# Six small experts a layer, and gate and up weights loaded in runs of four rows a partition

## The chip, the cores and the metric

The kernel runs on one core of a Trainium2 chip. The metric is the device time of one execution in microseconds. TensorE (PE) multiplies, VectorE (DVE), ScalarE (ACT) and GpSimd (POOL) do the elementwise work, and SyncE (SP) issues most of the DMAs.

## What is computed

Two layers of a decoder trunk over 512 tokens of width 1024. Each layer has a token mixer (an mLSTM beside sliding-window attention) and then a mixture of 16 experts, of which each token uses two. The change is in the experts alone:

```python
def _grouped_moe(h, w_router, router_bias, w_gate, w_up, w_down):
    ...
    gates = jnp.sum(jax.nn.one_hot(idx, N_EXPERTS, dtype=jnp.float32) * wts[..., None], axis=1)
    gates = gates.astype(h.dtype)
    y = jnp.zeros_like(t)
    for e in range(N_EXPERTS):
        act = jax.nn.silu(t @ w_gate[e]) * (t @ w_up[e])
        y = y + gates[:, e:e + 1] * (act @ w_down[e])
    return y.reshape(b, s, d)
```

`w_gate` and `w_up` are (layer, 16, 1024, 512), `w_down` is (layer, 16, 512, 1024), all float32: 6 MB an expert, 96 MB a layer.

## The kernel before

**One loop over experts.** `moe` runs positions 0 to 15 (line 1917). Each expert sees only the rows routed to it, gathered by an indirect DMA on POOL (`gather`, line 1395). Position 0 uses rows that are at hand; 1 to 15 have a tile `X` of up to 128 rows, one row a partition. Positions 3 to 14 are filled at run time: `order_experts` sorts these twelve experts by their row counts, and the ones with the fewest rows go to the positions in `SMALL`, the others to the rest (`RANK`, `perm`). What does not fit a position (more than 128 rows, or more than 64 at a small one) is left to an overflow block behind the loop. On these inputs it runs in layer 1 alone, for one expert with 146 rows.

**Large and small.** A small position works on 64 rows with plain float32 products: `gateup_small` computes gate and up side by side in two column groups of 64 (`gu`, line 1472), `down_small` the two halves of the down projection likewise (`downs`, line 1498). A large position works on 128 rows in three passes: every weight chunk is split into a high part (ACT, line 1548) and a low part (DVE, line 1549), and `mm3` (lines 116 to 118) sums three products. Its down projection is split in the same way if the position is in `DN` (`split_down`, lines 1457 and 1458), else it is plain float32 (line 1605).

**Order.** For each e the code writes gate and up of e, with the transposes of the previous expert's activations (`aT`) between their halves; then `turn(e + 1)`, which transposes the next expert's gathered rows to `XT` on PE, with `X` as the loaded operand and the identity as the moving one (line 1450 small, 1515 large); then down of e - 1. When a small expert follows one in `DN`, `gateup_small` splits two of that expert's four down blocks early. At e = 14 both down(13) and down(14) are written. A scheduler places the instructions of each engine from this order and its own estimates.

**Loads.** `up_gate` and `dn` list six chunks of 1 MB an expert (128 partitions of 2048 floats), gate and up of the next expert ahead of down of this one. They go through a ring of 12 buffers (`rot`, line 1366); SP issues a chunk when its buffer is free (`load`, line 1381). A chunk of gate or up holds 512 rows of 512 floats: partition p gets rows p, 128 + p, 256 + p and 384 + p, four runs of 2 KB. A down chunk holds 256 rows of 1024 floats, two runs of 4 KB.

Of the kernel before, what the change touches and what calls it, by code (L numbers as in the profile page):

```python
# [48 lines left out]
PQ = 2  # L49
SORTED = range(3, 15)  # L50
NSORT = len(SORTED)
SMALL = (4, 6, 8, 10, 12)
RANK = {}
for _e in SORTED:
    RANK[_e] = SMALL.index(_e) if _e in SMALL else len(SMALL) + sum(1 for _f in SORTED if _f < _e and _f not in SMALL)
DN = (1, 3, 5, 7, 9, 11, 13)
FR = 2
NPI = 2
MP = ((5, 2), (5, 2))
# [20 lines left out]
def tile_trunk(ctx, tc, x, c, w_ada, b_ada, w_norm1, w_in, conv_w, conv_b, b_igate, b_fgate, w_mnorm,  # L80
# [3 lines left out]
    V, A, G, T, SP = nc.vector, nc.scalar, nc.gpsimd, nc.tensor, nc.sync  # L84
# [13 lines left out]
    def ps(name="ps"):  # L98
        return pp.tile([128, 512], F32, tag="ps", name=name)
# [20 lines left out]
    def queue(*ins):  # L120

        for a, b in zip(ins, ins[1:]):
            tc.add_manual_dep(b.ins, a.ins.name, mybir.DependencyInfo(mybir.DependencyClass.NoSync,
                                                                      mybir.DependencyReason.DATA), reason="queue")
# [8 lines left out]
    ident = con.tile([128, 128], F32, name="ident")  # L133
# [1199 lines left out]
    def moe(l, raw2, rt):  # L1333
# [7 lines left out]
        X = [mp.tile([128, D], F32, name=f"X{i}", bufs=1) for i in range(2)]  # L1341
# [8 lines left out]
        regs = {}  # L1350

        def block(w, e, r0, nr):

            def f():
                if e not in RANK:
                    return w[l, e, r0:r0 + nr, :].rearrange("(a p) n -> p a n", p=128)
                if e not in regs:
                    r = RANK[e]
                    regs[e] = nc.values_load(perm[:, r:r + 1], engines=[ET.SP], min_val=SORTED[0], max_val=SORTED[-1])
                return w[l, ds(regs[e], 1), r0:r0 + nr, :].rearrange("o (a p) n -> p (o a) n", p=128)  # L1360
            return f, nr // 128

        def up_gate(e):
# [20 lines left out]
        def pair_of_chunks():  # L1384
            load(nch["got"] + len(rot))
            nch["got"] += 2
            return [loaded.popleft(), loaded.popleft()]

        def col(e):

            return SORTED[0] + RANK[e] if e in RANK else e

        def gather(e):
            n, c = 64 if e in SMALL else 128, col(e)
            G.indirect_dma_start(out=X[e % 2][:n], out_offset=None, in_=h2d[l],  # L1395
                                 in_offset=bass.IndirectOffsetOnAxis(ap=gidx0[:n, e - 1:e] if e < 3 else gidx[:n, c:c + 1], axis=0),
                                 bounds_check=S - 1, oob_is_err=False)
# [32 lines left out]
        def order_places():  # L1430

            V.memset(sml, 0.0)
            V.tensor_scalar(sml[:, sorted_], rank[:, :NSORT], float(len(SMALL)), None, op0=OP.is_lt)
            pr = oscr[:, :2 * TB * NE].rearrange("p (a b) -> p a b", b=NE)
# [8 lines left out]

        stt = {}

        def turn_small(e):
            XT = mpx.tile([128, D], F32, tag="XT", name="XT", bufs=2)[:, :512]
            p = ps("XT")
            for i in range(8):
                T.transpose(p[:, i * 64:(i + 1) * 64], X[e % 2][:64, i * 128:(i + 1) * 128], ident[:64, :64])  # L1450
            A.copy(XT, p)
            stt["XT", e] = XT.rearrange("p (a b) -> p a b", a=8)

# [7 lines left out]
        def gateup_small(e, mid):  # L1461

            XT = stt["XT", e]
            p = ps("gu")
            for half in range(2):
                if half and mid is not None:
                    mid()
                chs = pair_of_chunks()
                for i in range(4):
                    kb = 4 * half + i  # L1470
                    for g in range(2):
                        stt["gl"] = T.matmul(p[g * 64:g * 64 + 64], XT[:, kb], chs[g][:, i], start=kb == 0, stop=kb == KB - 1)  # L1472
            if e - 1 in DN:
                stt["wd", e - 1] = pair_of_chunks()
                stt["sd", e - 1] = [split_down(e - 1, fb) for fb in range(2)]
                stt["early"] = stt["sv"]
            a_ = mp.tile([128, DE], F32, name="act")
            A.activation(a_[64:128], p[0:64], AF.Silu)
            stt["mul", e] = V.tensor_mul(a_[0:64], p[64:128], a_[64:128])
            stt["act", e] = a_  # L1480
# [26 lines left out]
        def turn(e, XT=None):  # L1507
            if e in SMALL:
                return turn_small(e)
            if XT is None:  # L1510
                XT = [mpx.tile([128, D], F32R, tag="XT", name=n, bufs=2).rearrange("p (a b) -> p a b", a=8) for n in ("XTh", "XTl")]
            for q in range(2):
                p = ps("XT")
                for i in range(4):
                    T.transpose(p[:, i * 128:(i + 1) * 128], X[e % 2][:, (4 * q + i) * 128:(4 * q + i + 1) * 128], ident)  # L1515
                h_ = XT[0][:, 4 * q:4 * q + 4].rearrange("p a b -> p (a b)")
                A.copy(h_, p)
                o = V.tensor_sub(XT[1][:, 4 * q:4 * q + 4].rearrange("p a b -> p (a b)"), p, h_)
                if "early" in stt:
                    queue(stt.pop("early"), o)  # L1520
            stt["XT", e] = XT
# [30 lines left out]
        def gateup(e, mid=None):  # L1552
            if e in SMALL:
                return gateup_small(e, mid)
            XT = stt["XT", e]
            pg, pu = ps("gate"), ps("up")
            for half in range(2):
                if half and mid is not None:
                    mid()
                chs = [None] * 2 if e == 0 and half == 0 else pair_of_chunks()  # L1560
                for p, ch in zip((pg, pu), chs):
                    for j in range(2):
                        wh, wl = first.pop(0) if first else pair(ch, j)
                        for a in range(2):
                            kb = 4 * half + 2 * j + a
                            stt["gl"] = mm3(p, XT[0][:, kb], XT[1][:, kb], wh[:, a], wl[:, a], kb == 0, kb == KB - 1)
            a_ = mp.tile([128, DE], F32, name="act")
            A.activation(a_, pg, AF.Silu)
            stt["mul", e] = V.tensor_mul(a_, pu, a_)
            stt["act", e] = a_  # L1570

        def turn_act(e):
            if e in SMALL:
                return turn_act_small(e)
            a_ = stt["act", e]
            p = ps("aT")
            for i in range(4):
                T.transpose(p[:, i * 128:(i + 1) * 128], a_[:, i * 128:(i + 1) * 128], ident)
            if e in DN:
                aT = wsp.tile([128, D], F32R, tag="acc", name="aT", bufs=1).rearrange("p (k a b) -> p k a b", k=2, a=4)  # L1580
                h_, l_ = [aT[:, k].rearrange("p a b -> p (a b)") for k in range(2)]
                A.copy(h_, p)
                V.tensor_sub(l_, p, h_)
                stt["aT", e] = aT
                return
            aT = wsp.tile([128, D], F32, tag="acc", name="aT", bufs=1)[:, :512].rearrange("p (a b) -> p a b", a=4)
            A.copy(aT.rearrange("p a b -> p (a b)"), p)
            stt["aT", e] = aT

        def down(e):  # L1590
# [7 lines left out]
            for fb in range(4):  # L1598
                if e in DN:
                    wh, wl = sd.pop(0) if sd else split_down(e, fb)  # L1600
                for q in range(2):
                    if e in DN:
                        mm3(pd[q], aT[:, 0, fb], aT[:, 1, fb], wh[:, q], wl[:, q], fb == 0, fb == 3)
# [87 lines left out]
        def over_chunk(e, i, pool):  # L1691
            v = pool.tile([128, 2048], F32, tag="raw", name="oW")
            if i:
                G.tensor_copy(v[:, 0:2], g2[:, 0:2])
            w, r0, nr = ((w_gate_e, 0, 512), (w_up_e, 0, 512), (w_gate_e, 512, 512), (w_up_e, 512, 512),
                         (w_down_e, 0, 256), (w_down_e, 256, 256))[i]
            a = nr // 128
            SP.dma_start(v.rearrange("p (a b) -> p a b", a=a),
                         w[l, ds(e, 1), r0:r0 + nr, :].rearrange("o (a p) n -> p (o a) n", p=128))
            return v.rearrange("p (a b) -> p a b", a=a)  # L1700

        def over_block(chs, first=[], mid=None):
# [206 lines left out]
        a, v = turn_first(splits)  # L1909
# [57 lines left out]
        with none.Else():  # L1967
            with tc.If(n0 == 1) as one:
                tail(True)
            with one.Else():  # L1970
                V.tensor_scalar(ovl, ovl, 1.0, None, op0=OP.add)
                with tc.For_i(0, n0, 1):
                    e = over_rows()
# [4 lines left out]
                    for t in range(TB):  # L1978
                        for i in range(2):
                            p = ps("rows")  # L1980
# [182 lines left out]
```

## Time and profile before

| | us |
|---|---|
| median of 3 runs | 1422.01 (1420.73 to 1426.65) |
| the profiled execution | 1422.47 |
| its span in the trace | 1420.5 |
| PE busy | 1329.5 (94%) |
| DVE busy | 1005.1 (71%) |
| ACT busy | 678.4 (48%) |
| POOL busy | 204.8 (14%) |
| DMA, mean over the span | 257 GB/s |

The busy shares are means over the whole span. The experts of layer 0 lie at 420 to 712 us, those of layer 1 some 669 us later with the same pattern; the rest is the mixers and projections. The rows below are all from layer 0's experts but one.

### The profile page before, as it was taken

The numbers are of one execution on the slowest core, as the hardware profiler recorded it, in microseconds if no ns is written. First come the engines' busy times: TensorE is split into PE (matmuls) and PEld (weight loads), VectorE is DVE, ScalarE is ACT, GpSimd is POOL, SyncE is SP. The second block draws the span as 40 slices with busy tenths as digits, with TensorE's granted clock in tenths as the row PEclk, the third lists the DMA queues.
The fourth block names the chain that finished last, engine by engine and source line by source line (L and its number), as shares of the span: only waits on it lengthen the run. The fifth ranks groups of instructions, "written<-read, shape, count | busy, mean of one in ns | idle before, by whom it ended". The sixth has DMA issues, their size and how long they took to land.

```text
span 1420.5 us, 18468 instructions
## 1 busy us (share of the span) xinstructions
PE 1329.5 (94%) x6407; PEld 975.3 (69%) x6407; DVE 1005.1 (71%) x1941; ACT 678.4 (48%) x1184; POOL 204.8 (14%) x250
## 2 busy tenths in 40 slices
PE   2999999999989999999989999999998999999894
PEld 2776777778876756656568777777887666665662
DVE  5687756778679856767767566656958966766767
ACT  4345345454236645545356335435524655554552
POOL 7500020010011111110230000001001111211033
PEclk8999999999999999999999999999999999999997
DMA  9565465576868999999744434456577899999982
GB/s 312 202 219 177 133 246 178 178 232 184 294 218 286 360 376 390 376 370 395 281 158 149 148 97 142 149 194 176 184 261 250 290 351 389 382 375 384 392 317 84
DMA packets 166498, 365.08 MB, mean 257 GB/s; under 512 B 10549, under 2 KB 41517, under 8 KB 166136
## 3 DMA queue, kind: packets, MB, share of 16 engines
q1 hardware_dynamic: 152928, 327.71, 65.5%
q0 software_dynamic: 12752, 33.92, 7.0%
q10 hardware_dynamic: 712, 2.14, 0.5%
q8 instruction: 54, 0.88, 0.2%
q14 instruction: 52, 0.43, 0.1%
HBM read 346.27 MB, written 26.78 MB: 263 GB/s over the span
## 4 chain that ended last, share of the span: by engine, by line
PE 80%; DVE 11%; DMA 5%; issue 2%; ACT 1%; another core or an unknown queue 0%; SPq 0%; POOL 0%; DVEq 0%; ACTq 0%; POOLq 0%
PE winT L116 7%; PE winT L118 6%; PE winT L117 6%; PE gu L1472 5%; PE down L1605 3%; PE gate L117 3%; PE gate L118 3%; PE up L117 3%; PE gate L116 3%; PE up L118 3%; PE up L116 3%; PE downs L1498 2%; PE out L116 2%; PE out L118 2%; PE out L117 2%; DMA raw<-in_w_ada_dram 2%
## 5 line engine op out<-in xcount | busy, mean ns | idle before, releaser
L1548 ACT CAST wh<-raw 128x1024 fp32r<-128x1024 f32 x168 | 175.3, 1051 | 95.8 <-PE gate L118 65.6
L1549 DVE TENSOR_TENSOR wl<-raw,wh 128x1024 fp32r<-128x1024 f32 x168 | 201.5, 1223 | 23.5 <-ACT wh L1548 22.9
L116 PE MATMUL winT<-hh,wh 128*128 128x512 f32 x416 | 168.3, 405 | 0.5 <-DVE P L882 0.5
L118 PE MATMUL winT<-hh,wl 128*128 128x512 f32 x416 | 165.7, 398 | 0.0
L117 PE MATMUL winT<-hl,wh 128*128 128x512 f32 x416 | 165.4, 398 | 0.0
L483 ACT CAST wh<-raw 128x1024 fp32r<-128x1024 f32 (+1 forms) x59 | 54.2, 930 | 141.2 <-PE winT L117 86.4
L278 DVE SCALAR_TENSOR_TENSOR acc<-raw,cs,acc 128x1024 f32<-128x1024 f32 x70 | 89.7, 1282 | 33.3 <-DMA raw<-in_w_ada_dram 32.7
L116 PEld LDWEIGHTS winT<-hh,wh 128*128 128x128 f32 x416 | 79.1, 190 | 25.0 <-issue 5.1
L118 PEld LDWEIGHTS winT<-hh,wl 128*128 128x128 f32 x416 | 79.1, 190 | 18.5
L117 PEld LDWEIGHTS winT<-hl,wh 128*128 128x128 f32 x416 | 79.3, 191 | 17.7 <-DVE hl L463 0.3
L484 DVE TENSOR_TENSOR wl<-raw,wh 128x1024 fp32r<-128x1024 f32 (+1 forms) x57 | 60.4, 1068 | 27.8 <-ACT wh L483 27.8
L117 PE MATMUL gate<-wl,XTh 128*128 128x512 f32 x176 | 73.3, 417 | 5.8 <-DVE wl L1549 5.8
L116 PE MATMUL gate<-wh,XTh 128*128 128x512 f32 x176 | 72.4, 412 | 3.0 <-ACT XTh L1536 2.6
L1458 DVE TENSOR_TENSOR wl<-raw,wh 128x1024 fp32r<-128x1024 f32 x56 | 66.8, 1221 | 10.8 <-ACT wh L1457 10.8
L1472 PE MATMUL gu<-raw,XT 128*64 128x512 f32 x320 | 74.4, 596 | 0.0
L116 PE MATMUL up<-wh,XTh 128*128 128x512 f32 x176 | 69.8, 396 | 3.0 <-ACT wh L1548 3.0
L117 PE MATMUL up<-wl,XTh 128*128 128x512 f32 x176 | 70.8, 402 | 1.9 <-DVE wl L1549 1.9
L1395 POOL DMA_INDIRECT X<-h2d,gidx x30 | 38.0, 1266 | 238.8 <-PE XT L1515 103.6
L118 PE MATMUL gate<-wh,XTl 128*128 128x512 f32 x176 | 71.0, 404 | 0.5
L118 PE MATMUL up<-wh,XTl 128*128 128x512 f32 x176 | 69.6, 395 | 0.0
L329 POOL DMA_DIRECT2D modd<-adarow x8 | 4.2, 531 | 407.0 <-DVE adarow L328 407.0
L1457 ACT CAST wh<-raw 128x1024 fp32r<-128x1024 f32 x56 | 57.0, 1048 | 11.2 <-PE down L118 5.9
(529 smaller groups left out, 3035.9 us busy)
## 6 DMA issues: line engine op xcount, KB each, us to landing
raw<-in_w_down_e_dram SPq DMA_DIRECT2D x64, 1024.0 KB, 14.5
raw<-in_w_gate_e_dram SPq DMA_DIRECT2D x62, 1024.0 KB, 15.3
raw<-in_w_up_e_dram SPq DMA_DIRECT2D x62, 1024.0 KB, 14.0
raw<-in_w_ada_dram SPq DMA_DIRECT2D x40, 1024.0 KB, 5.1
raw<-in_w_in_dram SPq DMA_DIRECT2D x30, 1024.0 KB, 5.4
sch<-in_w_ada_dram SPq DMA_DIRECT2D x32, 256.0 KB, 6.4
raw<-in_w_out_dram SPq DMA_DIRECT2D x8, 1024.0 KB, 6.6
yk<-y2d SPq DMA_DIRECT2D x8, 1024.0 KB, 16.1
```

The source lines that it names most:

```text
L116: T.matmul(o, lh, rh, start=start, stop=False)
L117: T.matmul(o, lh, rl, start=False, stop=False)
L118: return T.matmul(o, ll, rh, start=False, stop=stop)
L278: V.scalar_tensor_tensor(self.acc, ch[:, a], cs[:, kb:kb + 1], self.acc, op0=OP.mult, op1=OP.add)
L483: A.copy(wh[:, :, a:b], src)
L484: (G if "first" in st else V).tensor_sub(wl[:, :, a:b], src, wh[:, :, a:b])
L1457: A.copy(wh.rearrange("p a b -> p (a b)"), src)
L1458: stt["sv"] = V.tensor_sub(wl.rearrange("p a b -> p (a b)"), src, wh.rearrange("p a b -> p (a b)"))
L1472: stt["gl"] = T.matmul(p[g * 64:g * 64 + 64], XT[:, kb], chs[g][:, i], start=kb == 0, stop=kb == KB - 1)
L1548: A.copy(wh, src)
L1549: stt["split"] = E.tensor_sub(wl, src, wh)
L1605: T.matmul(pd[q], aT[:, fb], wd[fb // 2][:, fb % 2, q * 512:(q + 1) * 512], start=fb == 0, stop=fb == 3)
```

## The change

`SMALL` goes from five positions to six, on the odd positions 3 to 13; `DN` follows, so that every large position from 1 to 14 is split and none is plain but 0's and 15's. Gate and up chunks from position 1 on are loaded with four adjacent rows on each partition, 4p to 4p + 3: one run of 8 KB in place of four of 2 KB. The contraction index of a block is then every fourth row, so the transposes of `X` read every fourth column (`run`), with 16 bytes from one element to the next. The overflow block does the same.

```diff
-SMALL = (4, 6, 8, 10, 12)
+SMALL = (3, 5, 7, 9, 11, 13)
...
-DN = (1, 3, 5, 7, 9, 11, 13)
+DN = (1, 2, 4, 6, 8, 10, 12, 14)
...
+                runs = e and nr == 512
                 if e not in RANK:
-                    return w[l, e, r0:r0 + nr, :].rearrange("(a p) n -> p a n", p=128)
+                    return w[l, e, r0:r0 + nr, :].rearrange("(p a) n -> p a n" if runs else "(a p) n -> p a n", p=128)
...
-                return w[l, ds(regs[e], 1), r0:r0 + nr, :].rearrange("o (a p) n -> p (o a) n", p=128)
+                return w[l, ds(regs[e], 1), r0:r0 + nr, :].rearrange("o (p a) n -> p (o a) n" if runs else "o (a p) n -> p (o a) n", p=128)
...
+        def run(x, kb):
+
+            return x[:, kb // 4 * 512:kb // 4 * 512 + 512].rearrange("q (p a) -> q a p", a=4)[:, kb % 4]
...
-                T.transpose(p[:, i * 64:(i + 1) * 64], X[e % 2][:64, i * 128:(i + 1) * 128], ident[:64, :64])
+                T.transpose(p[:, i * 64:(i + 1) * 64], run(X[e % 2][:64], i), ident[:64, :64])
...
-                    T.transpose(p[:, i * 128:(i + 1) * 128], X[e % 2][:, (4 * q + i) * 128:(4 * q + i + 1) * 128], ident)
+                    T.transpose(p[:, i * 128:(i + 1) * 128], run(X[e % 2], 4 * q + i), ident)
...
-                         w[l, ds(e, 1), r0:r0 + nr, :].rearrange("o (a p) n -> p (o a) n", p=128))
+                         w[l, ds(e, 1), r0:r0 + nr, :].rearrange("o (p a) n -> p (o a) n" if a == 4 else "o (a p) n -> p (o a) n", p=128))
```

**Order on PE, early in layer 0.** `down` is the product of a down projection (its two halves by number), `X` the gathered rows, `gu` a small expert's gate and up.

Before (the plain down of expert 2 ends the first rows):

```order
L1605 MATMUL down_4506<-raw,aT 128x512
L1605 MATMUL down_4507<-raw,aT 128x512
L1472 MATMUL gu<-raw,XT 64x512 x8
L1578 MATMUL aT<-ident,act 128x128 x4
L1472 MATMUL gu<-raw,XT 64x512 x8
L1515 MATMUL XT<-ident,X_3822 128x128 x8
L116 MATMUL down_4599<-wh,aT 128x512
```

After, PE with the split down of expert 1, `gu` of expert 3, `aT` of expert 2 and the transposes for expert 4:

```order
L117 MATMUL down_4326<-wl,aT 128x512
L118 MATMUL down_4326<-wh,aT 128x512
L1477 MATMUL gu<-raw,XT 64x512 x8
L1583 MATMUL aT<-ident,act 128x128 x4
L1477 MATMUL gu<-raw,XT 64x512 x8
L1520 MATMUL XT<-ident,X_3821 128x128 x8
L116 MATMUL down_4450<-wh,aT 128x512
```

The pair of a large and a small expert begins one position earlier, and the down ahead of it is one in three passes.

**Order on DVE, late in the layer.** `Y` is the weighed result, `aT` and `XTl` low parts of transposed activations and rows, `act` the activation of a small expert, `wl` at line 1458 (1463 after) the low part of a down block.

Before, DVE behind `downs` of expert 10:

```order
L1502 TENSOR_TENSOR Y<-downs,g_3190 64x512 x2
L1583 TENSOR_TENSOR aT<-aT 128x512
L1518 TENSOR_TENSOR XTl<-XT,XTh 128x512
L1479 TENSOR_TENSOR act<-gu,act 64x512
L1458 TENSOR_TENSOR wl<-raw,wh 128x1024 x2
L1518 TENSOR_TENSOR XTl<-XT,XTh 128x512
```

After, DVE behind `downs` of expert 9, and the same five rows behind `aT` stand again behind `downs` of expert 11:

```order
L1507 TENSOR_TENSOR Y<-downs,g_3190 64x512 x2
L1588 TENSOR_TENSOR aT<-aT 128x512
L1523 TENSOR_TENSOR XTl<-XT,XTh 128x512
L1484 TENSOR_TENSOR act<-gu,act 64x512
L1463 TENSOR_TENSOR wl<-raw,wh 128x1024 x2
L1523 TENSOR_TENSOR XTl<-XT,XTh 128x512
L1463 TENSOR_TENSOR wl<-raw,wh 128x1024 x2
L1612 TENSOR_TENSOR Y<-down_5490,g_3190 128x512
L1612 TENSOR_TENSOR Y<-down_5491,g_3190 128x512
```

The sequence `XTl`, `act`, two `wl`, `XTl` stood once in a layer and stands twice now. Elsewhere in the small experts both programs have `act` first, then both `XTl`, with some `wl` ahead of them.

**Order on DVE, at the end of the loop.** `osf` to `otok` are short steps for the overflow, `wl` at line 1549 (1554 after) the low part of a gate or up block.

Before, DVE with the last splits of down 13, the results of 13, two gate splits of 15 and the results of 14:

```order
L1458 TENSOR_TENSOR wl<-raw,wh 128x1024
L1651 CAST orv<-own 128x8
L1458 TENSOR_TENSOR wl<-raw,wh 128x1024
L1607 TENSOR_TENSOR Y<-down_5990,g_3190 128x512
L1607 TENSOR_TENSOR Y<-down_5991,g_3190 128x512
L1549 TENSOR_TENSOR wl<-raw,wh 128x1024 x2
L1607 TENSOR_TENSOR Y<-down_6049,g_3190 128x512
L1607 TENSOR_TENSOR Y<-down_6050,g_3190 128x512
```

After, DVE behind `downs` of 13, with the splits and the results of down 14, which is now split:

```order
L1588 TENSOR_TENSOR aT<-aT 128x512
L1463 TENSOR_TENSOR wl<-raw,wh 128x1024 x2
L1665 TENSOR_SCALAR osf<-oslot 128x1
L1666 TENSOR_TENSOR osl<-oslot,osf 128x1
L1667 TENSOR_REDUCE ow<-oslot 128x1
L1669 TENSOR_SCALAR osl<-osl 128x1
L1689 TENSOR_SCALAR ogi<-osl 128x1
L1670 CAST osf<-osl 128x1
L1671 TENSOR_TENSOR otok<-osf,firsts 128x4
L1463 TENSOR_TENSOR wl<-raw,wh 128x1024 x2
L1612 TENSOR_TENSOR Y<-down_5979,g_3190 128x512
L1612 TENSOR_TENSOR Y<-down_5980,g_3190 128x512
L1554 TENSOR_TENSOR wl<-raw,wh 128x1024 x8
```

Four splits and the overflow's short steps moved ahead of the last results, and the first gate splits of expert 15 behind them.

## Rows read from the trace of the kernel before

**Rows 1.** The page: its first line, and the last row of part 2, the GB/s that the DMA engines moved in 40 equal slices of the span (35.5 us each).

```profile
span 1420.5 us, 18468 instructions
...
GB/s 312 202 219 177 133 246 178 178 232 184 294 218 286 360 376 390 376 370 395 281 158 149 148 97 142 149 194 176 184 261 250 290 351 389 382 375 384 392 317 84
```

**Rows 2.** The windows view of two stretches of layer 0's experts. Columns: window (us), its length, busy us of PE, PEld, DVE, ACT and POOL (each with its count), granted clock, DMA share, GB/s.

```profile
550.00:600.00 50.00, 50.00 (x243) 29.57 (x242) 30.84 (x34) 24.56 (x31) 8.61 (x7) 1.00 1.04 377
600.00:650.00 50.00, 46.79 (x223) 30.05 (x223) 33.36 (x41) 25.77 (x32) 7.45 (x5) 1.00 1.01 378
```

**Rows 3.** The timeline of PE in layer 0. Columns: start, time to the end of the last one (us), engine, line, operation, out<-in, stationary and moving shape, count. The first row is expert 2's plain down; the rest is expert 7 (large, split) with expert 8 (small), and the last row the next large expert's start.

```profile
488.92 7.13 PE L1605 MATMUL down<-raw,aT 128*128 128x512 f32 x16
...
540.26 0.40 PE L116 MATMUL gate<-wh,XTh 128*128 128x512 f32 x1
...
552.77 3.65 PE L1498 MATMUL downs<-raw,aT 128*64 128x512 f32 x16
556.25 3.60 PE L1472 MATMUL gu<-raw,XT 128*64 128x512 f32 x16
559.79 0.66 PE L1578 MATMUL aT<-ident,act 128*128 128x128 f32 x4
...
563.96 1.09 PE L1515 MATMUL XT<-ident,X 128*128 128x128 f32 x8
564.80 0.47 PE L116 MATMUL down<-wh,aT 128*128 128x512 f32 x1
...
570.37 0.40 PE L116 MATMUL gate<-wh,XTh 128*128 128x512 f32 x1
```

**Rows 4.** The timeline of the loads that SP issues (start us; the second number runs over both issues of a row), at two places two pairs apart, the first of two down chunks each; then the DMA view of 540 to 625 us: issues, KB of each, median us from issue to landing.

```profile
533.94 2.72 SPq L1381 DMA_DIRECT2D raw<-in_w_down_e_dram  x2
...
609.88 3.51 SPq L1381 DMA_DIRECT2D raw<-in_w_down_e_dram  x2
...
raw<-in_w_down_e_dram SPq DMA_DIRECT2D x8, 1024.0 KB, 16.0
```

**Rows 5.** The DMA view of three short windows. First 552 to 556 us: all packets, then queue q1 (the loads; packets, MB, share of 16 engines); then q1 in 656 to 658 us; then q0 in 194 to 198 us, a stretch in which q0 stores to HBM.

```profile
DMA packets 778, 1.55 MB, mean 387 GB/s; under 512 B 22, under 2 KB 22, under 8 KB 778
...
q1 hardware_dynamic: 778, 1.55, 104.6%
...
q1 hardware_dynamic: 217, 0.82, 103.4%
...
q0 software_dynamic: 267, 1.47, 88.1%
```

**Rows 6.** The timeline from 600 to 636 us (down of expert 11, `gu` of expert 12): rows of PE, then of ACT, then of DVE. In brackets the idle time before a row and what ended it.

```profile
600.48 0.40 PE L116 MATMUL gate<-wh,XTh 128*128 128x512 f32 x1
...
618.74 7.08 PE L1472 MATMUL gu<-raw,XT 128*64 128x512 f32 x30
627.57 0.73 PE L116 MATMUL down<-wh,aT 128*128 128x512 f32 x2 [1.75 <-ACT wh L1457]
...
628.83 0.50 PE L117 MATMUL down<-wl,aT 128*128 128x512 f32 x1 [0.33 <-DVE wl L1458]
...
633.01 0.50 PE L117 MATMUL down<-wl,aT 128*128 128x512 f32 x1 [1.14 <-DVE wl L1458]
...
635.42 0.40 PE L116 MATMUL gate<-wh,XTh 128*128 128x512 f32 x1
...
625.86 0.59 ACT L1478 ACTIVATE act<-gu 64x512 f32<-64x512 f32 x1 [6.32 <-PE gu L1472]
...
629.14 2.00 ACT L1457 CAST wh<-raw 128x1024 fp32r<-128x1024 f32 x2 [0.68 <-DMA raw<-in_w_down_e_dram]
...
630.61 1.22 DVE L1646 TENSOR_TENSOR osel<-opos,iof 128x1024 bf16<-128x1024 f32 x1
```

**Rows 7.** The timeline of PE from the start of expert 14's gate to the start of expert 15's, and a window in it (columns as in Rows 2).

```profile
651.83 0.50 PE L116 MATMUL gate<-wh,XTh 128*128 128x512 f32 x1
654.65 0.80 PE L117 MATMUL gate<-wl,XTh 128*128 128x512 f32 x1 [2.32 <-DVE wl L1549]
...
683.78 0.48 PE L116 MATMUL gate<-wh,XTh 128*128 128x512 f32 x1
...
655.00:658.00 3.00, 3.00 (x8) 2.33 (x8) 1.87 (x2) 0.81 (x1) 0.38 (x1) 0.52 1.03 410
```

**Rows 8.** Transposes and weight loads: PE's timeline at 552.20; then the weight loads of line 1450 and of line 1515 (count: least/median/most ns, where in the span); then the group of the weight loads of split down projections (busy us, mean ns of one | idle before).

```profile
552.20 0.64 PE L1450 MATMUL XT<-ident,X 64*128 64x64 f32 x7
...
L1450 PEld LDWEIGHTS XT<-ident,X x80: 136/138/140, 478.6 to 1272.4; 64*128 64x128 f32 x80
...
L1515 PEld LDWEIGHTS XT<-ident,X x168: 137/140/143, 435.8 to 1366.9; 128*128 128x128 f32 x168
...
L116 PEld LDWEIGHTS down<-wh,aT 128*128 128x128 f32 x112 | 20.9, 188 | 9.3 <-ACT wh L1457 5.3
```

**Rows 9.** Groups of DVE instructions by line and shape: count | busy us, mean ns of one | idle before and what ended it.

```profile
L1549 DVE TENSOR_TENSOR wl<-raw,wh 128x1024 fp32r<-128x1024 f32 x168 | 201.5, 1223 | 23.5 <-ACT wh L1548 22.9
...
L1502 DVE TENSOR_TENSOR Y<-downs,g 64x512 f32<-64x512 f32 x20 | 13.8, 688 | 19.2 <-PE downs L1498 19.0
...
L1583 DVE TENSOR_TENSOR aT<-aT 128x512 fp32r<-128x512 f32 x14 | 9.7, 691 | 30.3 <-ACT aT L1582 30.3
...
L1660 DVE TENSOR_SCALAR osf<-oslot 128x1 f32<-128x1 f32 x4 | 0.6, 148 | 0.0
```

## The prediction, made before the changed kernel was run

> **What bounds the kernel now.** First the page: the GB/s slices [rows 1] stand at 360 to 395 in two stretches of the span, one for each layer's experts, and far lower elsewhere. Then the windows inside such a stretch [rows 2]: PE is busy for 50.00 of 50 us at a granted clock of 1.00, while the DMA share is already 1.04. So the expert stage has two limits close together: PE's instruction stream sets the end of each expert, and the weight transfers run at their full rate under it. DVE at 30.84 of 50 us has room on average, and matters only where PE waits for one of its splits.
>
> Next PE's timeline [rows 3], to price the units that the change exchanges. From 540.26 to 570.37 one large expert with a split down projection and one small expert take 30.11 us together: a **pair**. Small: `downs` 552.77 to 556.25 (3.48), half of `gu` 556.25 to 559.79 (3.54) and as much again, its transposes 0.64 [rows 8] and 0.40 of `aT`: 11.6 us. The rest, 18.5 us, is the large expert, whose split down takes 564.80 to 570.37 = 5.57 us. A large expert with a plain down pays 7.13 us for it [rows 3], so 20.0 in all.
>
> Then the loads, since 1 MB chunks must arrive in time [rows 4]. A down chunk issued at 533.94 with the median landing of 16.0 us is there at 549.9, 14.9 us before its use at 564.80 [rows 3]. Two pairs later one issued at 609.88 is there at 625.9, 1.7 us before its use at 627.57 [rows 6]. The **lead** falls by 6.6 us a pair. A second way gives the same: a pair loads 2 x 6.29 MB and moves 1.57 MB of rows (gather and put of 128 + 64 rows of 4 KB), 14.15 MB at 377 GB/s [rows 2] = 37.5 us against 30.1 of PE, 7.4 a pair. Reckoned back at 6.6, the lead is about 28 us in the first of the five pairs.
>
> **The change part by part.** *Six small experts.* Experts 1 to 14 of a layer were 7 large with split down, 2 large with plain down (20.0 each) and 5 small. Now they are 8 large, all split, and 6 small. One pair of 30.1 thus takes the place of two experts of 40.0: **-9.9 us a layer** on PE, which is the path. ACT and DVE gain a small expert's short work and lose a large one's 8 casts and 8 subtractions (1223 ns each [rows 9]); both lie under PE.
>
> *The order late in the layer.* Once in each layer of before (down of expert 11 beside `gu` of expert 12) the splits of the down weights come behind the silu and the second half of XTl on DVE, and PE shows it: gaps of 1.75, 0.33 and 1.14 us, and 600.48 to 635.42 = 34.94 us for a pair, 4.83 above the steady 30.11 [rows 6]. Of it a chunk that came 0.68 us late and the 1.22 us `osel` ahead of the last split are extras. In the new program that order stands twice, at down 10 and at down 12, without the `osel` ahead of the splits. I take the three gaps, 3.2 us, for each: 6.4 - 4.8 = **+1.6 a layer**.
>
> *The end of the experts.* Down 14 was plain and is now split, so four more splits stand on DVE between the small expert's results and the last large expert's first weights. Before, 651.83 to 683.78 held a gap of 2.32 us (PE waited for `wl`), after which the clock was granted at 0.52 for 3 us, worth 3 x 0.48 = 1.4 us [rows 7]. The whole stretch holds 26.2 us of PE's units (gate and up 11.4, transposes 0.84, two `aT` 1.3, downs 5.57 and 7.13), so its stalls came to 5.8. After, from the end of `downs` 13, DVE has two Y (1.4), `aT` (0.7), four splits (4.9) and seven short steps (1.0), then, 1 us after the last split, two Y again and the first gate split (1.4 + 1.2) [rows 9]: 11.6 us, for which PE has one `aT` and one split down, 6.2. That leaves a stall of 5.4, or 6.8 if the clock falls again. **0 a layer**, with -0.4 to +1.0.
>
> *Gate and up in 8 KB runs.* Bytes and issues stay the same; the rows on a partition become one run of 8 KB. No row of before has a weight load in such runs, so I bound it by what the packets of each size took [rows 5]. With packets of 2.0 KB on average q1 moved 1.55 MB in 104.6% of 4 us of 16 engines: 23.2 GB/s an engine. With 3.8 KB (mostly down): 0.82 MB in 103.4% of 2 us, 24.8. With stores of 5.5 KB on average: 1.47 MB in 88.1% of 4 us, 26.1. A gate or up chunk is 65.5 KB an engine: 2.82 us at the first rate, 2.51 at the last, so 0 to -0.31 each; with eight in a pair 0 to -2.5. I take -2.5, since throughput rises with size in both steps. This pays only where PE would wait. The lead of 28 us now falls for six pairs: by 4.1 each it ends its fifth fall at 7.5, so PE never waits for DMA; by 6.6 it is at -5. So the term is **0** on the path: the runs pay for the sixth pair.
>
> The Trainium skill's page "DMA: Bandwidth & Descriptors" (section "Where 436 GB/s comes from") says that for HBM to SBUF a limit of about 358 GB/s binds; by that rule longer runs would give nothing. The rows already stand above it, at 387 GB/s with 2 KB packets [rows 5].
>
> *Strided transposes.* PE's transposes of gathered rows load X as weights; they now read every fourth column. They number 96 of 64 rows (6 experts x 8 x 2 layers) and 152 of 128 rows (9 x 8 x 2, and 8 of the overflow). No strided load stands in the trace. Today a small one's load takes 138 ns with a step of at most 0.57/7 = 81 ns from one to the next, a large one's 140 ns with 0.84/8 = 105 ns [rows 8, 3]; the slowest load of another form is 188 ns [rows 8]. Bounds: 0; the slow form, +50 ns, 248 x 0.05 = +12.4; and a load at a quarter of the rate, priced below. I take +50 ns for the 96 small ones, whose step is short, and next to nothing for the large, where more time stands between two loads: **+5 us** in all.
>
> A page speaks against this part: the Trainium skill, "Advanced Engine Details and Errata", section "Memory Cachelines", has lines of 16 bytes in SBUF, wants "at least two hits on a cacheline" for full rate and calls a different line at each access a penalty. Float32 at a stride of four meets a new line each time; no run here shows what a PE read then costs. It is rival B.
>
> *Sum:* the profiled execution took 1422.47 us (0.46 above the median of 1422.01). Two layers of -9.9 + 1.6 + 0 = -16.6, and +5: **1410.9, say 1411**.
>
> **The rivals.** *A, the runs move no faster.* Then the sixth pair meets a lead of -5 us, and its splits need a chunk 1 to 2 us before PE does: 5 to 7 us of waits a layer, less what the two stretched pairs give the loads. 10 in two layers: **1421**. For it: the sharing of 16 engines may be limited by something else than the packet. Against: 4 KB packets are already quicker.
>
> *B, strided loads at a quarter rate.* Rows that arrive by one element of each 16 bytes could make a load four times as long; from the +50 ns above for half the rate that is +150 ns. Small 96 x 0.15 = 14.4; large 152 x 0.10 = 15.2 (45 ns of their step is slack): 1406 + 30 = **1436**, slower. It decides where each load costs over 0.1 us more. For it: PE has no slack to hide it [rows 2]. Against: 138 ns for a load with a step of 81 [rows 8] shows that loads overlap.
>
> *C, PE's new gaps are larger.* The late order and the end each cost 2 to 3 us a layer more than I take, for instance by a clock that falls twice: **1417 to 1420**, on the edge of no change.
>
> *D, it does not do what it says.* A small place holds 64 rows. If the sixth smallest of experts 3 to 14 held more, the overflow block would run and cost more than it saves. Counted from the reference on its inputs it holds 56 rows in layer 0 and 51 in layer 1; nothing is left for this one.
>
> **How the numbers follow.** Forecast 1411, with loads from 0 to +50 ns on all (1406 to 1418) and an end up to 2 us a layer better or worse: 0.68, nearly all faster. A 0.15, on the edge of same. B 0.10, mostly slower. C 0.07, same. About 0.5%, 7 us, is what a measurement of this kernel can tell from no change. Faster 0.72 (the forecast and the cheap part of A and C), same 0.19, slower 0.09. The range must leave out B and the far end of A: 1400 to 1424.
>
> **What would show it.** Steady pairs of 30.1 to 30.5 us and six of them a layer; the plain downs gone; two stretched pairs of about 33.3; gate and up landings no longer rising from pair to pair, and q1 packets of 8 KB moving over 25 GB/s an engine. Wrong would be a small expert's seven transposes over 1.2 us (B), PE gaps released by DMA in the fifth or sixth pair (A), or an end stretch of over 33 us (C).

## The result: slower by 0.8%, where 0.8% faster was forecast

The changed kernel took 1435.07 us (median of 5 runs, 1431.14 to 1436.04) beside 1423.63 for the kernel before: a ratio of 1.0083, 95% interval 1.0057 to 1.0108. The forecast was 1411 with 1400 to 1424.

The profiled execution has a longer span than before's [rows 1], by 12.8 us. Page of the changed kernel:

```profile
span 1433.3 us, 18403 instructions
```

In the middle of the experts the kernel runs nearly as forecast. Windows of the changed kernel (columns as in [rows 2]):

```profile
500.00:550.00 50.00, 50.00 (x238) 29.65 (x237) 30.60 (x32) 23.94 (x30) 7.91 (x6) 1.00 1.02 396
600.00:650.00 50.00, 45.90 (x210) 25.41 (x207) 24.12 (x31) 17.82 (x23) 7.53 (x6) 0.97 1.01 399
```

PE is full in the first, and the loads move more than before's 377 [rows 2]. In the second PE has 4.1 us of holes and a clock below 1.00; before had 3.2 us of holes there and a clock of 1.00. A pair, timeline of PE in the changed kernel (answers to [rows 3]):

```profile
493.73 0.40 PE L116 MATMUL gate<-wh,XTh 128*128 128x512 f32 x1
...
505.73 1.05 PE L1455 MATMUL XT<-ident,X 64*128 64x64 f32 x7
506.71 3.65 PE L1503 MATMUL downs<-raw,aT 128*64 128x512 f32 x16
...
517.90 1.23 PE L1520 MATMUL XT<-ident,X 128*128 128x128 f32 x8
518.88 0.47 PE L116 MATMUL down<-wh,aT 128*128 128x512 f32 x1
...
524.45 0.40 PE L116 MATMUL gate<-wh,XTh 128*128 128x512 f32 x1
```

It takes 30.72 us, 0.61 more than before. All of it lies in the transposes: seven of the eight small ones take 0.98 us in place of 0.57 (59 ns each), the eight large ones 0.98 in place of 0.84 (17 ns each). Their weight loads (answers to [rows 8]; least/median/most ns):

```profile
L1455 PEld LDWEIGHTS XT<-ident,X x96: 192/214/217, 472.7 to 1310.2; 64*128 64x128 f32 x96
...
L1520 PEld LDWEIGHTS XT<-ident,X x152: 195/211/219, 438.9 to 1380.3; 128*128 128x128 f32 x152
```

Late in the layer it goes wrong. Timeline of PE of the changed kernel, layer 0, from the start of expert 10's gate to the transposes of expert 15's activations, `aT` (answers to [rows 6, 7]; in brackets the idle time before and what ended it):

```profile
585.93 0.40 PE L116 MATMUL gate<-wh,XTh 128*128 128x512 f32 x1
...
614.39 0.73 PE L116 MATMUL down<-wh,aT 128*128 128x512 f32 x2 [1.75 <-ACT wh L1462]
615.65 0.50 PE L117 MATMUL down<-wl,aT 128*128 128x512 f32 x1 [0.53 <-DVE wl L1463]
621.03 0.40 PE L116 MATMUL gate<-wh,XTh 128*128 128x512 f32 x1
623.25 0.50 PE L117 MATMUL gate<-wl,XTh 128*128 128x512 f32 x1 [1.83 <-DVE wl L1554]
...
652.91 0.73 PE L116 MATMUL down<-wh,aT 128*128 128x512 f32 x2 [1.75 <-ACT wh L1462]
...
660.91 0.40 PE L116 MATMUL gate<-wh,XTh 128*128 128x512 f32 x1
663.13 0.50 PE L117 MATMUL gate<-wl,XTh 128*128 128x512 f32 x1 [1.83 <-DVE wl L1554]
...
688.54 0.40 PE L116 MATMUL gate<-wh,XTh 128*128 128x512 f32 x1
690.75 0.50 PE L117 MATMUL gate<-wl,XTh 128*128 128x512 f32 x1 [1.81 <-DVE wl L1554]
...
704.39 0.66 PE L1583 MATMUL aT<-ident,act 128*128 128x128 f32 x4 [0.85 <-DVE act L1574]
```

In the kernel before, gate 15 starts at 683.78 [rows 7] and has no such wait; its `aT`:

```profile
696.08 0.66 PE L1578 MATMUL aT<-ident,act 128*128 128x128 f32 x4 [0.85 <-DVE act L1569]
```

The fifth and the sixth pair take 35.10 and 39.88 us (36.44 and 38.29 in layer 1), against 30.72. Before paid 4.83 once a layer over its steady pair; here it is 13.5 and 13.3. Two engines show where the waits come from. ACT, then DVE, of the changed kernel, at the first of these places:

```profile
612.68 0.59 ACT L1483 ACTIVATE act<-gu 64x512 f32<-64x512 f32 x1 [6.36 <-PE gu L1477]
613.29 2.94 ACT L1462 CAST wh<-raw 128x1024 fp32r<-128x1024 f32 x3
```

```profile
614.37 2.36 DVE L1463 TENSOR_TENSOR wl<-raw,wh 128x1024 fp32r<-128x1024 f32 x2 [0.20 <-ACT wh L1462]
...
620.78 1.29 DVE L1612 TENSOR_TENSOR Y<-down,g 128x512 f32<-128x512 f32 x2 [1.06 <-PE down L118]
621.99 3.49 DVE L1554 TENSOR_TENSOR wl<-raw,wh 128x1024 fp32r<-128x1024 f32 x3
```

ACT stands idle for 6.36 us with the casts of the down weights queued behind a silu that needs the end of `gu`; PE, which has done its transposes earlier, then waits 1.75 us for the first cast. On DVE the two results `Y` need the end of the down projection (hence the 1.06 us), and the first low part of the next gate is queued behind them, so PE waits 1.83 us at that gate. The same wait returns at gate 14 (663.13) and gate 15 (690.75). On top comes the clock, in windows of the changed kernel (the granted clock is the third figure from the end):

```profile
624.00:627.00 3.00, 3.00 (x8) 2.33 (x8) 2.23 (x3) 1.04 (x1) 0.09 (x1) 0.51 1.04 427
...
655.00:658.00 3.00, 3.00 (x8) 2.35 (x8) 2.97 (x4) 1.04 (x1) 0.00 (x0) 0.50 1.01 416
```

Behind the wait at 623.25 and behind that at 652.91 PE runs at 1.2 GHz in place of 2.4 for some 3.4 us, 1.7 us lost each time. From gate 0 to gate 15 the kernel before shows one such fall in each layer [rows 7], the changed one three in layer 0 and four in layer 1. One of the three, at 429.5 us, stands early, at expert 0; one more, at 692.3, follows the wait at gate 15.

### The profile page after: what moved, and what is told of

Its sections match the earlier page's. It is cut to its first block, busy times and chain, and to the rows that moved or that the text cites. A ratio compares the mean times of both kernels' runs of the same rounds, so it can differ in the third digit from the quotient of the medians.

```text
span 1433.3 us, 18403 instructions
## 1 busy us (share of the span) xinstructions
PE 1337.5 (93%) x6391; PEld 977.2 (68%) x6391; DVE 996.5 (70%) x1931; ACT 669.9 (47%) x1174; POOL 203.5 (14%) x250
## 4 chain that ended last, share of the span: by engine, by line
PE 78%; DVE 11%; DMA 6%; ACT 2%; issue 2%; another core or an unknown queue 0%; SPq 0%; ACTq 0%; POOL 0%; DVEq 0%; POOLq 0%
PE gu L1477 6%; PE winT L116 5%; PE winT L117 5%; PE winT L118 5%; DMA raw<-in_w_ada_dram 3%; PE downs L1503 3%; PE gate L117 3%; PE up L117 3%; PE up L118 3%; PE up L116 3%; PE gate L118 3%; PE gate L116 3%; PE down L117 2%; PE out L116 2%; PE out L118 2%; PE out L117 2%
## 5 line engine op out<-in xcount | busy, mean ns | idle before, releaser
L1553 ACT CAST wh<-raw 128x1024 fp32r<-128x1024 f32 x152 | 159.2, 1050 | 89.3 <-PE gate L118 56.2
L1554 DVE TENSOR_TENSOR wl<-raw,wh 128x1024 fp32r<-128x1024 f32 x152 | 182.3, 1222 | 26.2 <-ACT wh L1553 25.3
L1477 PE MATMUL gu<-raw,XT 128*64 128x512 f32 x384 | 90.7, 596 | 0.0
L1463 DVE TENSOR_TENSOR wl<-raw,wh 128x1024 fp32r<-128x1024 f32 x64 | 76.4, 1221 | 12.9 <-ACT wh L1462 12.3
L117 PE MATMUL gate<-wl,XTh 128*128 128x512 f32 x160 | 66.9, 418 | 11.7 <-DVE wl L1554 11.7
L1462 ACT CAST wh<-raw 128x1024 fp32r<-128x1024 f32 x64 | 64.8, 1047 | 15.6 <-PE down L118 14.2
L1396 POOL DMA_INDIRECT X<-h2d,gidx x30 | 33.9, 1130 | 263.5 <-PE XT L1455 132.2
L116 PE MATMUL gate<-wh,XTh 128*128 128x512 f32 x160 | 66.3, 415 | 3.0 <-ACT XTh L1541 2.6
L116 PE MATMUL up<-wh,XTh 128*128 128x512 f32 x160 | 64.5, 403 | 3.0 <-ACT wh L1553 3.0
L117 PE MATMUL up<-wl,XTh 128*128 128x512 f32 x160 | 65.0, 406 | 1.9 <-DVE wl L1554 1.9
L118 PE MATMUL gate<-wh,XTl 128*128 128x512 f32 x160 | 65.2, 408 | 0.5
L118 PE MATMUL up<-wh,XTl 128*128 128x512 f32 x160 | 64.3, 402 | 0.0
```

The costliest lines, as they stand in the source:

```text
L116: T.matmul(o, lh, rh, start=start, stop=False)
L117: T.matmul(o, lh, rl, start=False, stop=False)
L118: return T.matmul(o, ll, rh, start=False, stop=stop)
L1462: A.copy(wh.rearrange("p a b -> p (a b)"), src)
L1463: stt["sv"] = V.tensor_sub(wl.rearrange("p a b -> p (a b)"), src, wh.rearrange("p a b -> p (a b)"))
L1553: A.copy(wh, src)
```

## The experiments

"Loop" is the time from the first gate product of expert 0 to that of expert 15 in layers 0 and 1, read off PE's timeline of each profiled execution. "Tail" is the time from there to the `aT` of expert 15, which takes in the wait at gate 15. Every ratio is to the kernel before.

| | time, us | ratio (95%) | loop, us | tail, us |
|---|---|---|---|---|
| before | 1423.6 | | 263.2, 263.1 | 12.3, 12.3 |
| changed | 1435.1 | 1.0083 (1.0057 to 1.0108) | 265.8, 267.4 | 15.8, 14.3 |
| e1 six only | 1426.5 | 1.0027 (1.0008 to 1.0045) | 261.0, 261.0 | 14.3, 15.9 |
| e2 runs only | 1429.0 | 1.0040 (1.0023 to 1.0056) | 266.3, 266.4 | 12.3, 12.3 |
| e3 permuted rows | 1430.8 | 1.0065 (1.0040 to 1.0089) | 263.9, 263.7 | 15.8, 14.3 |
| e4 transposes behind `gu` | 1418.9 | 0.9967 (0.9944 to 0.9989) | 257.6, 257.4 | 15.9, 15.8 |
| e5 first split ahead | 1421.5 | 0.9994 (0.9979 to 1.0010) | 262.5, 261.6 | 12.7, 12.7 |
| e6 all three orders | 1401.5 | 0.9859 (0.9831 to 0.9887) | 253.8, 253.8 | 12.7, 12.7 |
| e7 as e6, old layout | 1408.9 | 0.9904 (0.9882 to 0.9925) | 257.0, 256.7 | 12.7, 12.7 |
| e8 before, three orders | 1423.0 | 1.0002 (0.9982 to 1.0022) | 263.4, 265.8 | 12.3, 12.3 |
| e9 as e6, permuted rows | 1402.9 | 0.9863 (0.9831 to 0.9894) | 251.2, 250.0 | 12.7, 12.7 |
| e10 as e6, 14 plain | 1403.9 | 0.9872 (0.9844 to 0.9901) | 252.7, 252.4 | 14.5, 14.5 |

Of the 12.8 us between the profiles of the changed kernel and of the one before, 6.9 are in the loops and 5.5 in the tails, by the wait at gate 15 and, in layer 0, a fall of the clock behind it. The rest of the span differs by 0.4 us between these two; over all runs it lies between 867 and 876 us, with the clock falling at other places in each, so it is not read further. What loops and tails gain or lose against the kernel before comes within 3 us of the change of time by the ratio in every run but e9 (-24.4 against -19.5).

**e1, the six positions alone.**

```diff
-SMALL = (4, 6, 8, 10, 12)
+SMALL = (3, 5, 7, 9, 11, 13)
-DN = (1, 3, 5, 7, 9, 11, 13)
+DN = (1, 2, 4, 6, 8, 10, 12, 14)
```

> The kernel before with the six small positions and the new list of split downs alone; weights in four runs of 2 KB and contiguous transposes as before. Three theories for the 24 us between the forecast and the changed kernel. ORDER: late in a layer the splits of the down weights and the first gate split stand too late on ACT and DVE (experts 9 to 15), PE waits some 2 us at each, and the granted clock falls behind the waits; the strided loads cost 8 us in all (0.6 us a pair, as the trace after shows). The order of instructions here is the same as in the changed kernel, so 1435 - 8 = 1427, and up to 1435 if the 2 KB loads fall behind PE in the last pair. LOADS: the strided loads cost the whole 24 us, in places the timeline hides: 1411. DMA: the 8 KB runs are what the sixth pair needs: over 1435, with PE waits that end on a DMA.

1426.5, as ORDER said; LOADS falls. Waits of PE in e1, 460 to 690 us (total, times, longest):

```profile
PE gate L117 <- DVE wl L1549: 5.5, 3, 1.8
PE down L116 <- ACT wh L1457: 5.2, 3, 1.8
PE down L117 <- DVE wl L1458: 1.4, 3, 0.5
```

They are the late waits of the changed kernel, and none ends on a DMA although the loads come in 2 KB runs. With these holes in PE the 8 KB runs buy nothing. Its loops are 2.1 to 2.2 us shorter than before's; the tails, 2.0 and 3.6 longer, take that back.

**e2, runs and strided transposes alone.**

```diff
-SMALL = (3, 5, 7, 9, 11, 13)
+SMALL = (4, 6, 8, 10, 12)
-DN = (1, 2, 4, 6, 8, 10, 12, 14)
+DN = (1, 3, 5, 7, 9, 11, 13)
```

> The changed kernel with the five small positions and the list of split downs of before: only the 8 KB runs and the strided transposes are new. ORDER: the late places are those of the kernel before, so only the loads are added: 80 small x 59 ns + 168 large x 18 ns, 4.7 + 3.0 = +7.7 on 1423.6: 1431. LOADS: 248 loads at 0.1 us, +24: 1447. DMA: the runs remove the 0.7 us wait for a chunk in the last pair of each layer and nothing else.

+5.7 us by the ratio (3.3 to 8.0) and +3.2 us a loop: again ORDER's price, not LOADS'. The late pair takes 35.5 us, before's 34.9 and the 0.6 of the transposes: with no wait of ACT for a down chunk left there, PE's gaps stayed.

**e3, contiguous transposes with 8 KB runs.**

```diff
-            V.tensor_mul(self.h[t][:, hs], xt[t, i], self.A2[:, hs])
+            V.tensor_mul(to_runs(self.h[t][:, hs]), by_runs(xt[t, i]), by_runs(self.A2[:, hs]))
...
-                T.transpose(p[:, i * 64:(i + 1) * 64], run(X[e % 2][:64], i), ident[:64, :64])
+                T.transpose(p[:, i * 64:(i + 1) * 64], X[e % 2][:64, i * 128:(i + 1) * 128], ident[:64, :64])
```

(and the like in the two adds of `B2` and in the large transposes; `by_runs` is `"q (p a) -> q a p"`, `to_runs` `"q (a p) -> q a p"`, both with a = 4.)

> The changed kernel, but the normed rows are stored with their columns already in the order of the runs (DVE and GpSimd read by a stride of four when they make them), so PE's transposes read contiguous columns while the weights come in 8 KB runs. ORDER: weight loads of transposes back at 138 ns, steady pairs at 30.1 us, about 8 us less than the changed kernel: 1427, up to 2 us more if the strided elementwise reads are slow. LOADS: 1411. DMA: as ORDER, without PE waits that end on a DMA.

The steady pairs are back at 30.1 us, but the time fell by less than 8 us; 1430.8 is not told apart from the changed kernel's 1435. The loops are 2.7 to 2.9 us above e1's with the same waits, but the clock falls four times in each and twice in each of e1's, which is worth 3.4; the span less the loops is 1.6 longer. What the strided elementwise reads cost was not separated from the clock.

**e4, the transposes behind `gu`.**

```diff
-TGL = (0,)
+TGL = (0, 11, 13)
```

> The changed kernel with one number list longer: at experts 11 and 13 the next expert's transposes are issued behind the last product of gate and up, as they stand in the early pairs; on DVE the order then is silu product, two down splits, both XTl, two splits, first gate split, results. ORDER: the gap of 1.8 us at gate 12 and gate 14 goes and the 1.75 us ones shrink by the 1 us of transposes, and with them one or two falls of the clock at 1.7 us each: 5 to 9 us a layer less, 1417 to 1425. LOADS: nothing: 1435. DMA: nothing.

1418.9, within ORDER's range: one list of numbers turns 0.8% slower into 0.3% faster. Timeline of PE in e4, the place of 614.39 above:

```profile
610.97 1.23 PE L1520 MATMUL XT<-ident,X 128*128 128x128 f32 x8
...
612.79 0.73 PE L116 MATMUL down<-wh,aT 128*128 128x512 f32 x2 [0.59 <-ACT wh L1462]
...
620.05 0.39 PE L116 MATMUL gate<-wh,XTh 128*128 128x512 f32 x1
620.29 0.40 PE L117 MATMUL gate<-wl,XTh 128*128 128x512 f32 x1
```

The transposes cover 1 us of the wait, and the gate's second product follows without a gap: with the transposes moved, the first gate split stands ahead of `Y` on DVE too. So e4 sets two orders at once, and does not tell them apart. The loops are 9 us shorter a layer, with no fall of the clock in either; gate 15 keeps its wait (the tails).

**e5, the first gate split ahead of `Y`.** `YQ` is (12, 14, 15), `Y0` the first result, and `queue(a, b)` puts b behind a on its engine.

```diff
+                        if "Y0" in stt and e in YQ:
+                            queue(stt["split"], stt.pop("Y0"))
```

> The changed kernel with one dependency more on DVE: at experts 12, 14 and 15 the first low part of gate's weights stands ahead of the results of the down projection before it. The transposes stay where they were. ORDER, as it stands after four runs: the gap of 1.8 us (2.0 us of a gate's path) goes at each of the three, 6 us a layer, and with it one or two of the clock's falls at 1.7 us: 1435 - 12 to - 19, 1416 to 1423. A rival, SPLITS: these gaps only move into the down projection's last results, because DVE has no time left there, and PE waits for its results' buffers: over 1430.

1421.5, at the slow end of ORDER's range; SPLITS (over 1430) falls. The waits at gates 12 and 15 are gone (the tails show the second). At gate 14 one of the two `Y` went ahead of the split all the same, and a wait of 1.68 us stays.

**e6, both, and the early down splits ahead of the silu.** `SQ` is (11, 13), `sc` the second cast, `s_` the silu.

```diff
+            if e in SQ:
+                queue(stt["sc"], s_)
```

> The changed kernel with three orders set: transposes behind gate and up at experts 11 and 13, the first gate split ahead of the results at 12, 14 and 15, and at 11 and 13 the two early down splits ahead of the silu on ACT. ORDER: the loop of e4 took 257.5 us a layer; without the 2.0 us at gate 15, one clock fall there (1.7) and 1 to 2 us of waits for the down splits it takes 252 to 254: 1408 to 1411. SPLITS: as e4, 1419.

1401.5, 7 us better than expected, though the loops are as expected (253.8). The expectation counted the wait at gate 15 into the loop; it stands behind it, and the tails are 3.2 us a layer shorter than e4's, 6.4 in all. DVE, then the windows, of e6:

```profile
616.07 1.23 DVE L1558 TENSOR_TENSOR wl<-raw,wh 128x1024 fp32r<-128x1024 f32 x1
617.27 1.29 DVE L1618 TENSOR_TENSOR Y<-down,g 128x512 f32<-128x512 f32 x2
```

```profile
550.00:600.00 50.00, 50.00 (x231) 33.72 (x231) 33.39 (x35) 26.79 (x31) 7.59 (x7) 1.00 1.02 410
600.00:650.00 50.00, 50.00 (x233) 28.72 (x229) 32.02 (x40) 24.03 (x29) 6.89 (x6) 1.00 1.01 404
```

The split stands before `Y`, and PE is full to 650 us at full clock.

**e7, the same with the old layout.** The two `rearrange` strings and the two transposes as in the kernel before.

> As e6, but with the old layout: weights in four runs of 2 KB and contiguous transposes. Its pair is 30.1 us in place of 30.7 and has fewer gaps in which loads can catch up. ORDER with loads that keep pace: 8 us below e6, about 1401. DMA: the lead of the loads falls by 6.6 us a pair and is gone in the fifth or sixth: PE waits that end on a DMA, 5 to 7 us a layer, so 1411 to 1415, no better than e6; then the 8 KB runs earn in e6 what they cost.

1408.9, between the two numbers, but on DMA's side of e6: 6.4 us above it by the ratios and 3.1 us a loop, although its steady pairs are 0.6 us shorter. Timeline of PE, then waits of ACT (560 to 690 us), in e7:

```profile
639.13 3.71 PE L1479 MATMUL gu<-raw,XT 128*64 128x512 f32 x16 [0.43 <-DMA raw<-in_w_up_e_dram]
644.78 3.65 PE L1479 MATMUL gu<-raw,XT 128*64 128x512 f32 x14 [1.94 <-DMA raw<-in_w_up_e_dram]
```

```profile
ACT wh L1464 <- DMA raw<-in_w_down_e_dram: 14.3, 2, 8.5
```

With PE's holes gone, chunks come late: ACT waits 5.8 us for a down chunk in the fifth pair and 8.5 in the sixth, and behind each PE waits 1.2 us for a low part, besides the two waits above; e6 has no such row. The rate behind it, in the DMA views of 552 to 556 us, of e7 and then of e6 (376 and 404 GB/s over 500 to 600 us):

```profile
DMA packets 589, 1.47 MB, mean 368 GB/s; under 512 B 68, under 2 KB 68, under 8 KB 589
```

```profile
DMA packets 337, 1.66 MB, mean 415 GB/s; under 512 B 67, under 2 KB 67, under 8 KB 202
```

So the 8 KB runs are worth what they cost, and more, once PE no longer waits for its own neighbours.

**e8, the kernel before with the orders.** e7 with the old `SMALL` and `DN`, and the lists (0, 12), (13,) and (12,).

> The kernel before (five small positions, old layout) with the same three orders at its one late place (expert 12, and the first gate split at 13). ORDER: the late pair of 34.9 us falls to 31 or 32: 3 to 4 us a layer, 1416 to 1418. Against e7 it gives the six positions alone when both have the order: by the units 9.9 us a layer, less what the end of the loop costs.

No gain; the expectation missed. Its late pair still takes 34.1 us. PE of e8, 600 to 660 us:

```profile
624.88 3.65 PE L1479 MATMUL gu<-raw,XT 128*64 128x512 f32 x14 [0.84 <-DMA raw<-in_w_up_e_dram]
...
634.73 0.50 PE L119 MATMUL down<-wl,aT 128*128 128x512 f32 x1 [1.23 <-DVE wl L1465]
639.25 0.50 PE L119 MATMUL gate<-wl,XTh 128*128 128x512 f32 x1 [1.74 <-DVE wl L1558]
```

A chunk is late (ACT also waits 7.0 us for a down chunk), and the order of DVE did not become the early one: one of the two `Y` and the `osel` still stand ahead of the split for gate 13. What the order alone would be worth in the kernel before stays open.

**e9 and e10, towards a best version.** e9 is e6 with e3's rows; e10 is e6 with

```diff
-DN = (1, 2, 4, 6, 8, 10, 12, 14)
+DN = (1, 2, 4, 6, 8, 10, 12)
```

> e6 (8 KB runs, three orders) with the rows stored in permuted column order as in e3, so that transposes read contiguous columns. It has the transposes' 138 ns loads and the 8 KB runs at once. ORDER: the loop falls from 253.8 to about 249.6 a layer (0.6 us a pair and 0.2 us at each other large expert), less what the strided elementwise reads cost before the loop (e3's two stretches outside the loops were 3 us longer than e1's): 1401.5 - 8.4 + 3, about 1396. A rival, LOADS AGAIN: with 30.1 us a pair the 8 KB loads fall behind by 4 us a pair and PE waits on a DMA in the last pair: 1400.

> e6 with expert 14's down projection plain again (seven split downs). ORDER: down 14 takes 1.5 us more on PE, and the two waits for its splits (1.62 and 0.33 us) and the clock fall behind them (1.7) go: 2 us a layer less, 1397 to 1399. If PE then waits for its activations instead (0.7 us before the plain down of 14 in the kernel before), no change: 1401.

Neither is told apart from e6. e9's loops are 3.2 us shorter a layer, and no PE wait ends on a DMA, so LOADS AGAIN falls; the span less the loops is 7 us longer than e6's, and how much of that is the strided elementwise work was not separated. e10's loops are 1.3 us shorter, but its tails 1.8 longer: the expectation did not see that one `Y` would stand ahead of the first gate split again, and PE waits 1.47 us at gate 15. That is why there is no gain.

## Why the prediction was wrong, point by point

**Six small experts, -9.9 us a layer: held** as a unit price. A pair replaced two plain experts at the price read off, and e6 against the kernel before shows what is left when the waits are out: -9.3 us a loop with strided transposes in it. The sum at the end of this section, which uses the price, comes within 0.6 us of each layer.

**The order late in the layer, +1.6: the step that failed.** Right in place and in sign, it was mis-sized: 13.3 to 13.5 us a layer against before's 4.8, so +8.5 to +8.7. Three things were wrong. The term took off the old place whole, 4.8 us, and charged each new one with its three gaps alone, 3.2. I priced three gaps of the old late place and did not ask what else stood in another place in the new order. The rows of DVE for the changed kernel have both `Y` directly behind the down splits, and at the end of the loop all eight gate splits behind them; in the kernel before one gate split stands ahead of the `Y`. DVE before, behind down 11:

```profile
634.28 1.23 DVE L1549 TENSOR_TENSOR wl<-raw,wh 128x1024 fp32r<-128x1024 f32 x1
635.42 1.28 DVE L1607 TENSOR_TENSOR Y<-down,g 128x512 f32<-128x512 f32 x2
```

The other order is a wait of 1.8 us at each of gates 12, 14 and 15. And I gave the clock a term at the end alone, although in these traces waits of 1.6 to 2.3 us on PE are often followed by a fall worth 1.7 us. e4, e5 and e6 show the order as the cause: -16.5, -12.7 and -32 us against the changed kernel by their ratios, with nothing computed differently.

**The end of the experts, 0: failed by the same step.** From gate 14 to gate 15 the units of the new end (22.6 us) leave 5.0 us of stalls in layer 0's 27.63 us, against 5.8 before, and 7.8 in layer 1, where the clock falls twice, against 5.6. That alone would look about right. But this stretch ends ahead of the wait at gate 15, which my stall of 5.4 had counted in: with the tails, 3.5 and 2.0 us longer than before, the stalls are 8.5 and 9.8. What the 5.4 put at nothing is the wait at gate 14, ahead of `downs` of 13, and the falls of the clock. So the end costs +2.7 and +4.2 us a layer, where I gave -0.4 to +1.0.

**8 KB runs, 0 on the path: right here, and incomplete.** The loads moved 396 and 399 GB/s in the two windows above, and no PE wait ended on one; but e1 shows that 2 KB would have done as well beside these holes. The lead that I reckoned to run out at -5 us in the sixth pair ran out in e7, once the holes were gone.

**Strided transposes, +5: mis-sized.** 96 x 59 ns and 152 x 17 ns are 8.3 us; e1 against the changed kernel gives 8.0 by the ratios, e2 5.7 for its 7.7 (6.3 in its loops, where the clock falls as often as before). The load itself costs 73 ns more (138 to about 212), between the +50 taken and the +150 of rival B.

**In sum**, a layer: -9.9 (units) + 4.1 (strides) + 8.7 or 8.5 (order) + 2.7 or 4.2 (end) makes +5.6 in layer 0 and +6.9 in layer 1; loop and tail show +6.1 and +6.3. Rival B named about the right time, 1436, for a cause that made up 8 of its 30 us. Rival C had the mechanism, "PE's new gaps are larger", at 2 to 3 us a layer each (which adds up to 1419 to 1423, not to its 1417 to 1420), and a chance of 0.07. None of the three signs of being wrong appeared: the small transposes took 1.05 us, no PE wait ended on a DMA, and the ends took 27.6 and 30.4 us, since the waits lay in the late pairs and behind the end.

## What to carry to other kernels

Where a scheduler places the instructions, read the new order of each engine that feeds the bound one, row by row at the place where it differs, and give every instruction that stands behind a later-finishing one its wait. Then reckon with a clock fall behind each wait of some 2 us on PE (1.7 us here). When a stretch is timed to account for a change, let it end behind the last wait that the change moves: the loop here ended just ahead of one. A change that frees time on PE may only pay after its neighbours' orders are set anew: here the same change was 0.8% slower without and 1.4% faster with three orders, and only then did the faster loads matter.

## What the runs showed of the hardware

A float32 transpose whose loaded operand is read with a stride of four elements takes 211 to 214 ns for its weight load where a contiguous one takes 138 to 140, for 64 and for 128 rows alike; the step from one transpose to the next grew by 59 ns (64 rows) and 17 ns (128 rows). The Trainium skill's page "Advanced Engine Details and Errata" (section "Memory Cachelines") speaks of a penalty when each access meets another line; the trace agrees, and the size here is a half more, not a multiple.

The clock did not fall at every wait: at 614.39 a wait of 1.75 us and one of 0.53 left the following products at full speed, and the one of 1.83 at 623.25 did not; at 652.91 the first two were enough. In the two loops and tails of the changed kernel a fall followed 7 of the 12 waits of 1.6 us or more. Which it will be could not be read from the rows.
